# Turning rows into columns on TensorE in the opening of a fused conv and SwiGLU layer

## The chip, the cores and the metric

One NeuronCore of a Trainium2 chip runs the whole kernel as one program. The metric is the device time of one execution in microseconds; the median of the runs is used. The engines named below are TensorE (PE, with its weight loads shown apart as PEld), VectorE (DVE), ScalarE (ACT), GpSimd (POOL) and SyncE (SP), which here only issues DMAs.

## The reference

One layer, in float32, over 2048 tokens of width 1024. `c` is a vector of 1024 that turns into six vectors of shifts, scales and gates.

```python
c_act = silu(c)
sh_m, sc_m, g_m, sh_f, sc_f, g_f = split(c_act @ ada_w + ada_b, 6)
h = rms_norm(x, gain0) * (1 + sc_m) + sh_m          # over the 1024 features of a token
gate_b, gate_c, v = split(h @ w_in, 3)              # 1024 x 3072
h = (gate_b * causal_conv3(gate_c * v)) @ w_out     # 1024 x 1024
x = x + g_m * rms_norm(h, gain1)
h = rms_norm(x, gain2) * (1 + sc_f) + sh_f
g, u = split(h @ w_gate_up, 2)                      # 1024 x 5632
h = (silu(g) * u) @ w_down                          # 2816 x 1024
out = x + g_f * rms_norm(h, gain3)
```

## The kernel before

Features lie on partitions and tokens along the free axis. The 2048 tokens are two units of 1024, and a unit is two halves of 512 tokens (`tok` 0 and 1). Each matrix product is cut into 2 x 2 blocks and done with seven block products P1 to P7 in place of eight (Winograd's form of Strassen). A block product over 512 features is four steps `k` of 128, and a step is three matmuls of 128x512 in the fp32r format: the operands are split into an upper part (`high`, `upper`: a cast on ACT) and a lower part (`low`, `lower`: a subtraction on DVE), and high x high, low x high and high x low are added in PSUM.

The phases follow each other: in0, out0, in1, out1, gu0, down0, gu1, down1. Each phase is a list of slots, a slot being one block product of one group of output features. Work around the slots (loads, sums and splits of weights) is issued by due slots, some slots ahead. All instructions of an engine run in the order in which the program emits them: nothing overtakes on an engine.

The opening, `start()`, is written out by hand, because nothing is on the chip yet. It covers slots 0 to 12 of in0 in pieces and prepares the ones up to 18: P1 of five groups (slots 0 to 4), P2 of five groups (5 to 9), P7 of three (10 to 12); P6 (13 to 15), P5 (16 to 18), P3 and P4 of three groups follow from the general loop. The features of the unit are four tiles of 128 x 4 x 512: `a` and `b` are the lower and upper 512 features of the first token half, `c` and `d` those of the second half. P1 needs `a`, P2 needs `b`, P7 needs `e = a - c`, P6 needs `d - e`, P5 needs `c + d` (in whole fp32 words, without a split).

To make them, `start()` does these steps:

- `load_rows` brings the 512 rows of x of a half; `squares` adds up their squares on ACT; `factor` makes 1/rms of each row (`root`: a power on POOL and three small DVE steps) and puts them on the diagonals of four 128 x 128 blocks (`diagonal`, tile `r0d` or `r1d`); `spread` makes of them, with a product by ones, a tile whose every row holds the factors along the tokens (`rb`).
- `f.load("a")` to `f.load("d")` bring the same rows of x a second time, as columns, from a transposed copy in DRAM (`xt_d`). `mult` multiplies them by `rb` on DVE; `shift` applies scale and shift (`mA`, `mB`) on ACT; `upper` and `lower` split.
- The scales `mA` and shifts `mB` are made in quarters `q` of 256 features. `scales(q, i)` multiplies columns of `ada_w` (128 features on partitions, 1024 inputs along the free axis) by silu(c), spread over the partitions, and adds up along the free axis, in two DVE instructions of 512. `c_half` is that spread c, from two DMAs that read c once for every partition, and `Silu` on ACT. `shifts(q)` does the same sums on TensorE, as a product of one column of silu(c) with 256 features, eight steps; `turned(q)` copies the resulting row to SBUF and turns it into columns with two small transposes. `fold(q)` adds biases and gains.
- `advance("blocks" / "high" / "low" / "sums", i)` takes the loads, casts, subtractions and sums of the weights up to slot i.
- `products(first, ks, ns)` does steps `ks` of slots `first + n`; `follow` takes finished products out of PSUM.

Sixteen tiles of 2 KB a partition hold raw weights, seventeen of 8 KB hold the big operands, and PSUM has eight banks. Nearly every instruction shows line 78 in the profile, since one helper emits them all; rows are told apart by tile names (`in0a` is tile `a`; `ada` columns of ada_w; `ms` the column sums; `pms` the row sums in PSUM; `in0P` either an accumulator or a split weight; `wb` products of ones ahead of the work).

Of the kernel before, what the change touches and what calls it, by code (L numbers as in the profile page):

```python
# [49 lines left out]
def hybrid_conv_layer(  # L50
# [109 lines left out]
    mB = [const.tile([P, KD], F32, name=f"mB{i}") for i in range(2)]  # L160
# [12 lines left out]
    def mods_later(ms, pace):  # L173

        s2 = {(m, h): sb.tile([P, KD], F32, tag="ms", bufs=4, name=f"ms{m}_{h}") for m in ms for h in range(2)}
        for h in range(2):
            half = slice(h * CH, (h + 1) * CH)
            row = raw(f"c{ms[0]}_{h}")
            SP.dma_start(row, c_row[:, half].to_broadcast((P, CH)))
            todo = [(m, n) for m in ms for n in range(KD)]  # L180
            tiles = {}

            def load(i, half=half, todo=todo, tiles=tiles):
                if i < len(todo):
                    m, n = todo[i]
                    tiles[i] = raw(f"ada{m}_{half.start}_{n}")
                    SP.dma_start(tiles[i], ada[m - 1, n][:, half])

            load(0)
            yield pace  # L190
            load(1)
            yield pace
            A.activation(row, row, AF.Silu)
            load(2)
            yield pace
            for i, (m, n) in enumerate(todo):
                load(i + 3)
                t = tiles.pop(i)
                V.tensor_tensor_reduce(t, t, row, 1.0, 0.0, ALU.mult, ALU.add, col(s2[m, h], n))
                yield pace  # L200
# [865 lines left out]
    def start():  # L1066
        ph = phases[0]
        rb, mods, rows, xr = {}, {}, {}, {}
        f = Features(ph, from_xt(0), rb, 0)
        s2 = [sb.tile([P, KD], F32, tag="ms", bufs=4, name=f"ms1_{h}") for h in range(2)]  # L1070
# [9 lines left out]
        def load_scale(q):  # L1080

            t = mods[1, q] = big(f"ada1_{q}")
            for i in range(2):
                SP.dma_start(pair_of(t, i), two(ada[0, 2 * q + i]))
# [7 lines left out]
        sq = {}  # L1092

        def squares(tok, rs):
            if tok not in sq:
                sq[tok] = small(4, f"a{tok}")
            for r in rs:
                t = pair_of(xr[tok][r // 2], r % 2)
                A.activation(t, t, AF.Square, scale=1.0 / 32.0, accum_out=col(sq[tok], r))

        def factor(tok, meanwhile=lambda: None):
# [4 lines left out]
            meanwhile()  # L1106
            return diagonal(at_once(steps), f"r{tok}")

        def shifts(q):
            t = mods[0, q].rearrange("p a b -> p (a b)").rearrange("p (k n) -> p k n", k=KD)  # L1110
            rows[q] = bank(f"pms{q}")
            for k in range(KD):
                PE.matmul(rows[q][0:1, :256], col(cact, k), t[:, k, :], start=k == 0, stop=k == KD - 1)
# [4 lines left out]
        def scales(q, i):  # L1118
            for h in range(2):
                t = mods[1, q][:, 2 * i + h, :]  # L1120
                V.tensor_tensor_reduce(t, t, c_half[h], 1.0, 0.0, ALU.mult, ALU.add, col(s2[h], 2 * q + i))

        def fold(q):
            n = slice(2 * q, 2 * q + 2)
            t = small(2, f"mf{q}")
            V.tensor_tensor(t, s2[0][:, n], s2[1][:, n], ALU.add)
            V.tensor_tensor(t, t, vt[:, VB + KD + n.start : VB + KD + n.stop], ALU.add)
            V.scalar_tensor_tensor(mA[0][:, n], t, 1.0, vt[:, VG + n.start : VG + n.stop], ALU.add, ALU.mult)
            V.tensor_tensor(mB[0][:, n], rows[q][:, :2], vt[:, VB + n.start : VB + n.stop], ALU.add)

        def mult(key, k4):
            t = f.t[key][:, k4, :]
            V.tensor_tensor(t, t, rb[f.place[key][0]], ALU.mult)

        def shift(key, k4):
            t, k = f.t[key][:, k4, :], f.place[key][1] * 4 + k4
            A.activation(t, t, AF.Identity, bias=col(mB[0], k), scale=col(mA[0], k))
# [24 lines left out]
        load_scale(0)  # L1162
        load_shift(0)
        f.load("a")
        advance("blocks", 2)
        load_scale(1)
        load_shift(1)
        advance("blocks", 4)
        f.load("b")
        load_scale(2)  # L1170
        load_shift(2)
        advance("blocks", 7)
        load_shift(3)
        load_rows(1)
        load_scale(3)
        advance("blocks", 9)
        f.load("c")
        advance("blocks", 12)
        f.load("d")
# [12 lines left out]
        for _ in range(6):  # L1192
            PE.matmul(b, one, w, start=True, stop=True)


        squares(0, range(4))
        for h in range(2):
            A.activation(c_half[h], c_half[h], AF.Silu)
        dg = factor(0)
        rb[0] = spread(dg, "r0")  # L1200
        scales(0, 0)
        scales(0, 1)
        shifts(0)
        advance("high", 0)
        for k in range(3):
            mult("a", k)
        turned(0)
        fold(0)
        mult("a", 3)
        advance("low", 0)  # L1210
        for k in range(2):
            shift("a", k)
            upper("A11", k)
            lower("A11", k)
# [3 lines left out]
        scales(1, 0)  # L1218
        scales(1, 1)
        shifts(1)  # L1220
# [3 lines left out]
        turned(1)  # L1224
        fold(1)
        products(4, range(2), range(1))
        split("a", "A11", range(2, 4))
        products(0, range(2, 4))
        for k in range(4):
            mult("b", k)  # L1230
        shifts(2)
        scales(2, 0)
        scales(2, 1)
        products(3, range(2, 4), range(1))
        squares(1, range(2))
        turned(2)
        advance("high", 7)
        products(4, range(2, 4), range(1))
        advance("low", 7)
        squares(1, range(2, 4))  # L1240
        fold(2)
        shifts(3)
        v = small(4, "v1")
        V.tensor_scalar(v, sq[1], EPS, None, ALU.add)
        steps = root(v, "r1")
        next(steps)
        shift("b", 0)
        upper("A12", 0)
        scales(3, 0)
        lower("A12", 0)  # L1250
        shift("b", 1)
        upper("A12", 1)
        scales(3, 1)
        dg = at_once(steps)
        lower("A12", 1)
        turned(3)
        fold(3)
        dg = diagonal(dg, "r1")
        products(5, range(2), range(1))
        rb[1] = spread(dg, "r1")  # L1260
        products(6, range(2), range(1))
        advance("sums", 12)
        shift("b", 2)
        upper("A12", 2)
        mult("c", 0)
        lower("A12", 2)
        mult("c", 1)
        shift("b", 3)
        upper("A12", 3)
        lower("A12", 3)  # L1270
        follow(0, range(3))
        mult("c", 2)
        mult("c", 3)
        products(5, range(2, 4), range(2))
# [5 lines left out]
        products(7, range(4), range(1))  # L1280
        for k in range(4):
            shift("c", k)
# [3 lines left out]
        products(9, range(4), range(1))  # L1286

# [19 lines left out]
        e(3)  # L1307
        advance("low", 12)
        lower("S3", 2)
        lower("S3", 3)  # L1310
        products(10, range(2))
# [4 lines left out]
        for k in range(4):  # L1316
            mult("d", k)
            shift("d", k)
# [149 lines left out]
```

## Time and profile before

| | us |
|---|---|
| median of 3 runs | 1979.15 (1978.1 to 1981.15) |
| the profiled execution | 1980.41 |
| its span on the core | 1978.3 |
| PE busy | 1943.6 (98%) |
| DVE busy | 1465.0 (74%) |
| ACT busy | 869.4 (44%) |

The page splits the span into 40 slices of 49.5 us with one digit for each engine. The opening fills slice 1 and most of slice 2. The windows view gives the same for stretches of one's own choice; the timeline gives every instruction with start, length, and, in brackets, how long its engine had been idle and what ended that.

### The profile page before, as it was taken

The page shows a single profiled execution, that of the slowest core. Times are in us where ns is not written, and L with a number is a line of the kernel's source. Part 1 is how long each engine was busy: PE and PEld are TensorE (multiplying, and loading weights), DVE is VectorE, ACT ScalarE, POOL GpSimd, SP SyncE. Part 2 cuts the span into 40 slices and gives each one's busy share as a digit, 9 for nine tenths or more (in the row PEclk, how much of TensorE's full clock was granted, in tenths as well). Part 3 has the DMA queues.
Part 4 walks back from the last instruction along what each step waited for, and adds up shares of the span by engine and source line. Part 5 has one row for each costly group of instructions (what it writes and reads, how often), then busy time and mean ns, then how long its engine had stood idle before and what let it go on. Part 6 is the DMA issues. An engine that isn't in the chain of part 4 may idle for free.

```text
span 1978.3 us, 24971 instructions
## 1 busy us (share of the span) xinstructions
PE 1943.6 (98%) x8460; PEld 1575.3 (80%) x8460; DVE 1465.0 (74%) x2159; ACT 869.4 (44%) x1428; POOL 344.2 (17%) x224
## 2 busy tenths in 40 slices
PE   7899998999999999999999999999999999999998
PEld 3578886777888888888888888888888888888886
DVE  4898887988999776898776755686776655665466
ACT  4543446544345653443333444463333333344452
POOL 0012201311221211243332320120100100011010
PEclk9999998999999999999999999999999999999999
DMA  9369859859996773777666877577564342386634
GB/s 389 131 226 379 305 172 359 302 201 351 337 317 216 288 261 102 231 246 242 206 223 202 281 285 277 202 261 274 186 197 152 113 154 96 109 310 230 198 138 132
DMA packets 204463, 458.97 MB, mean 232 GB/s; under 512 B 22832, under 2 KB 38320, under 8 KB 197936
## 3 DMA queue, kind: packets, MB, share of 16 engines
q1 hardware_dynamic: 179712, 403.00, 59.3%
q10 hardware_dynamic: 24624, 54.40, 7.2%
q8 instruction: 66, 1.08, 0.2%
q14 instruction: 61, 0.50, 0.1%
HBM read 326.23 MB, written 131.07 MB: 231 GB/s over the span
## 4 chain that ended last, share of the span: by engine, by line
PE 88%; DMA 4%; DVE 4%; issue 2%; ACT 1%; SPq 0%; ACTq 0%; POOL 0%; POOLq 0%; DVEq 0%
PE gu0P L78 21%; PE gu1P L78 21%; PE down0P L78 11%; PE in1P L78 10%; PE in0P L78 10%; PE down1P L78 9%; PE out1P L78 4%; PE out0P L78 1%; DMA ada<-ada_d 1%; DMA in3b<-w_in_d 1%; DMA in0b<-xt_d 0%; DMA ident<-eye_d 0%; DMA in1b<-w_in_d 0%; DVE down1z L78 0%; DMA in2b<-w_in_d 0%
## 5 line engine op out<-in xcount | busy, mean ns | idle before, releaser
L78 DVE TENSOR_TENSOR gu1a<-gu1P,gu1a 128x512 f32<-128x512 f32 x63 | 43.5, 691 | 108.6 <-PE gu1P L78 108.6
L78 DVE TENSOR_TENSOR gu0a<-gu0P,gu0a 128x512 f32<-128x512 f32 x63 | 43.4, 688 | 70.0 <-PE gu0P L78 68.3
L78 POOL TENSOR_TENSOR gu1a<-gu1a 128x512 f32<-128x512 f32 x11 | 19.0, 1728 | 363.5 <-DVE gu1g11s L78 42.5
L78 ACT COPY gu1a<-gu1P 128x512 f32<-128x512 f32 x42 | 24.7, 588 | 98.6 <-PE gu1P L78 87.5
L78 POOL TENSOR_TENSOR nq<-nq,nq 128x512 f32<-128x512 f32 x28 | 42.7, 1525 | 132.8 <-ACT nq L78 128.1
L78 DVE CUSTOM_DVE_ANT_0 ada<-ada,c 128x512 f32<-128x512 f32 x80 | 60.1, 761 | 4.0 <-DMA ada<-ada_d 4.0
L78 ACT COPY gu0a<-gu0P 128x512 f32<-128x512 f32 x42 | 24.5, 587 | 84.6 <-PE gu0P L78 83.5
L78 ACT COPY gu1g<-gu1P 128x512 f32<-128x512 f32 x24 | 14.1, 588 | 92.9 <-PE gu1P L78 92.9
L78 POOL TENSOR_TENSOR down0q<-down0q,down0q 128x512 f32<-128x512 f32 x14 | 23.9, 1704 | 144.1 <-ACT down0q L78 144.0
L78 ACT COPY gu0g<-gu0P 128x512 f32<-128x512 f32 x24 | 14.1, 588 | 77.2 <-PE gu0P L78 77.2
L78 POOL TENSOR_TENSOR gu0a<-gu0a 128x512 f32<-128x512 f32 x11 | 18.3, 1660 | 170.9 <-ACT gu0a L78 50.4
L78 POOL TENSOR_TENSOR down1q<-down1q,down1q 128x512 f32<-128x512 f32 x10 | 16.1, 1610 | 148.7 <-ACT down1q L78 148.6
L78 DVE TENSOR_TENSOR gu1g<-gu1P,gu1g 128x512 f32<-128x512 f32 x24 | 16.6, 691 | 27.5 <-ACT gu1g L78 26.0
L78 DVE TENSOR_TENSOR down2P<-down2P,down2P 128x512 fp32r<-128x512 f32 x14 | 11.9, 853 | 28.6 <-ACT down2P L78 28.6
L78 ACT ACTIVATE gu1a<-gu1a 128x512 f32<-128x512 f32 x42 | 26.6, 633 | 13.4 <-DVE xo L78 6.0
L78 POOL TENSOR_TENSOR out1q<-out1q,out1q 128x512 f32<-128x512 f32 x14 | 22.1, 1579 | 52.3 <-ACT out1q L78 52.3
L78 ACT ACTIVATE gu0a<-gu0a 128x512 f32<-128x512 f32 x42 | 26.6, 632 | 10.4 <-DVE gu0a L78 9.0
L78 POOL TENSOR_TENSOR out0q<-out0q,out0q 128x512 f32<-128x512 f32 x14 | 23.0, 1640 | 46.5 <-ACT out0q L78 46.5
L78 DVE TENSOR_TENSOR xx<-xx,zz 128x512 f32<-128x512 f32 x32 | 29.1, 909 | 1.1
L78 ACT ACTIVATE nq<-xx 128x512 f32<-128x512 f32 x32 | 20.2, 631 | 17.2 <-DVE xx L78 13.9
L78 DVE TENSOR_TENSOR gu0g<-gu0P,gu0g 128x512 f32<-128x512 f32 x24 | 16.5, 689 | 14.4 <-ACT gu0g L78 13.0
L78 ACT ACTIVATE xr<-xr 128x512 f32<-128x512 f32 (+1 forms) x24 | 18.5, 772 | 16.3 <-DMA xr<-x_d 15.3
(3225 smaller groups left out, 6723.5 us busy)
## 6 DMA issues: line engine op xcount, KB each, us to landing
ada<-ada_d SPq DMA_DIRECT2D x64, 256.0 KB, 5.9
act0A<-gu0a SPq DMA_DIRECT2D x33, 256.0 KB, 3.6
act1A<-gu1a SPq DMA_DIRECT2D x33, 256.0 KB, 2.4
ada<-ada_d SPq DMA_DIRECT2D x16, 512.0 KB, 9.4
zz<-z SPq DMA_DIRECT2D x32, 256.0 KB, 5.3
xx<-xt_d SPq DMA_DIRECT2D x32, 256.0 KB, 5.3
x<-xx ACTq DMA_DIRECT2D x32, 256.0 KB, 5.3
down0S<-act0S SPq DMA_DIRECT2D x8, 1024.0 KB, 6.9
```

What stands on the lines that cost most here:

```text
L78: return tc.keep_in_program_order(f(*args, **kwargs))
```

## The change

The opening no longer reads the transposed copy of x, nor c spread from DRAM.

- `turn(key, k)` takes the rows of x as the stationary operand and the diagonal of the factors as the moving one: four products of 128 x 128 x 128 give one step `k` of a feature tile, turned into columns and multiplied by 1/rms, in a PSUM bank. `shift` reads that bank. `mult`, `spread`, `rb` and the loads of `xt_d` in the opening go.
- `spread_c` makes the spread silu(c) with two products by ones.
- `squares` now writes to a tile `junk`, since the rows are needed later; the fourth row tile of a half is squared on DVE (`squares_of_last`).
- The shifts of the first quarter are still done by `shifts(0)` on TensorE, in two parts; those of the other three quarters on DVE with `sums_of(0, n)`, as the scales are with `sums_of(1, n)`. `fold` now goes by single k from k = 2 on. For this `ada_d` holds all six vectors, not five.
- The order of the steps is written anew.

```diff
-    c_half = [tmp(f"c1_{h}")[:, :CH] for h in range(2)]
-    for h in range(2):
-        A.dma_start(c_half[h], c_row[:, h * CH : (h + 1) * CH].to_broadcast((P, CH)))
...
+        def squares_of_last(tok):
+            t, a = pair_of(xr[tok][1], 1), small(2, f"a{tok}h")
+            for h in range(2):
+                V.tensor_tensor_reduce(pair_of(junk, 1)[:, h, :], t[:, h, :], t[:, h, :], 1.0 / 1024.0, 0.0,
+                                       ALU.mult, ALU.add, col(a, h))
+            V.tensor_tensor(col(sq[tok], 3), col(a, 0), col(a, 1), ALU.add)
...
+        def turn(key, *ks):
+            tok, kk = f.place[key]
+            for k in ks:
+                b = turned_x[key, k] = bank(f"x{key}{k}")
+                for r in range(4):
+                    PE.matmul(b[:, r * P : (r + 1) * P], xr[tok][r // 2][:, 2 * (r % 2) + kk, k * P : (k + 1) * P],
+                              dg[tok][:, r * P : (r + 1) * P], start=True, stop=True)
+
+        def spread_c():
+            dg = [diagonal(cact[:, 4 * h : 4 * h + 4], f"c{h}") for h in range(2)]
+            for h in range(2):
+                c_half[h] = tmp(f"c1_{h}")[:, :CH]
+            for h in range(2):
+                b = bank(f"c{h}b")
+                PE.matmul(b, one, dg[h][:, :CH], start=True, stop=True)
+                yield A.copy(c_half[h], b)
...
+        def sums_of(m, n):
             for h in range(2):
+                t = mods[m, n // 2][:, 2 * (n % 2) + h, :]
+                V.tensor_tensor_reduce(t, t, c_half[h], 1.0, 0.0, ALU.mult, ALU.add, col(s2[h], m * KD + n))
+
+        def fold(n0, n1, by_rows=True):
+            g = lambda t: t[:, : 2 * KD].rearrange("p (m n) -> p m n", m=2)[:, int(by_rows) :, n0:n1]
+            V.tensor_tensor(g(mods1), g(s2[0]), g(s2[1]), ALU.add)
+            V.tensor_tensor(g(mods1), g(mods1), g(vt[:, VB : VB + 2 * KD]), ALU.add)
+            V.scalar_tensor_tensor(mA[0][:, n0:n1], mods1[:, KD + n0 : KD + n1], 1.0, vt[:, VG + n0 : VG + n1],
+                                   ALU.add, ALU.mult)
+            if by_rows:
+                V.tensor_tensor(mB[0][:, n0:n1], rows[n0 // 2][:, : n1 - n0], vt[:, VB + n0 : VB + n1], ALU.add)
...
+            A.activation(f.t[key][:, k4, :], turned_x.pop((key, k4)), AF.Identity, bias=col(mB[0], k),
+                         scale=col(mA[0], k))
...
         load_rows(0)
-        load_scale(0)
         load_shift(0)
-        f.load("a")
+        load_columns(1, 0)
         advance("blocks", 2)
...
+        load_columns(1, 3)
+        load_columns(0, 3)
         load_rows(1)
```

The new order of the steps, from the products of ones on (all of it new text; unchanged steps left out after `e`):

```python
        ones(2)
        steps = spread_c()
        squares(0, range(2)); next(steps); squares(0, range(2, 3)); next(steps)
        squares_of_last(0)
        ones(4)
        factor(0)
        shifts(0, range(4)); turn("a", 0); shifts(0, range(4, 8)); turned(0); turn("a", 1, 2)
        sums_of(1, 0); sums_of(1, 1); advance("high", 0); fold(0, 2); advance("low", 0)
        for k in range(2):
            split("a", "A11", (k,)); advance("high", 1 + k); advance("low", 1 + k)
        products(0, range(2)); turn("a", 3)
        advance("high", 4); advance("low", 4)
        products(3, range(2), range(1)); products(4, range(2), range(1))
        for k in range(2, 4):
            sums_of(0, k); sums_of(1, k); fold(k, k + 1, False); split("a", "A11", (k,))
        products(0, range(2, 4)); turn("b", 0, 1)
        sums_of(0, 4); sums_of(1, 4); fold(4, 5, False); shift("b", 0); upper("A12", 0)
        sums_of(0, 5); sums_of(1, 5); lower("A12", 0); fold(5, 6, False); shift("b", 1); upper("A12", 1)
        products(3, range(2, 4), range(1)); advance("high", 7); products(4, range(2, 4), range(1))
        lower("A12", 1); advance("low", 7)
        products(5, range(2), range(1)); turn("b", 2); sums_of(0, 6); sums_of(1, 6)
        products(6, range(2), range(1)); fold(6, 7, False); squares(1, range(2))
        shift("b", 2); upper("A12", 2); sums_of(0, 7); sums_of(1, 7); lower("A12", 2)
        turn("b", 3); fold(7, 8, False); shift("b", 3); upper("A12", 3)
        squares(1, range(2, 3)); lower("A12", 3); squares_of_last(1); factor(1)
        advance("sums", 12)
        products(5, range(2, 4), range(1)); turn("c", 0); shift("c", 0); follow(0, range(3))
        products(6, range(2, 4), range(1)); turn("c", 1); shift("c", 1)
        follow(3, range(2)); advance("high", 9); follow(5, range(1)); advance("low", 8); follow(6, range(1))
        products(7, range(2), range(1)); turn("c", 2, 3); shift("c", 2); shift("c", 3)
        products(7, range(2, 4), range(1)); advance("low", 9)
        products(8, range(4), range(1)); follow(7, range(1)); products(9, range(4), range(1))
        turn("d", 0, 1)
        # e(0) to e(3) as before; then shift("d", 0), shift("d", 1), turn("d", 2, 3),
        # shift("d", 2), shift("d", 3), and on as before without mult("d", k)
```

More of the change, by code (lines that the diff above doesn't have):

```diff
@@ L1217, in start @@
         products(0, range(2))
[L1218 to L1220 removed]
+        turn("a", 3)
         advance("high", 4)
@@ L1241, in start @@
[L1241 to L1258, printed above, removed]
         products(5, range(2), range(1))
-        rb[1] = spread(dg, "r1")
+        turn("b", 2)
@@ L1271, in start @@
+        for _ in factor(1):
+            pass
+        advance("sums", 12)
+        products(5, range(2, 4), range(1))
+        turn("c", 0)
+        shift("c", 0)
         follow(0, range(3))
-        mult("c", 2)
-        mult("c", 3)
-        products(5, range(2, 4), range(2))
+        products(6, range(2, 4), range(1))
+        turn("c", 1)
+        shift("c", 1)
         follow(3, range(2))
```

165 lines of the change are left out of this document (83 added, 82 removed).

## The prediction

> **What bounds the kernel now.** I read the page first (busy shares, then the slices), then the chain of waits, then the windows and the timeline of the first 130 us.
>
> ```profile
> span 1978.3 us, 24971 instructions
> PE 1943.6 (98%) x8460; PEld 1575.3 (80%) x8460; DVE 1465.0 (74%) x2159; ACT 869.4 (44%) x1428; POOL 344.2 (17%) x224
> ...
> PE   7899998999999999999999999999999999999998
> ...
> DVE  4898887988999776898776755686776655665466
> ...
> PEclk9999998999999999999999999999999999999999
> DMA  9369859859996773777666877577564342386634
> ```
>
> TensorE is full except in slices 1, 2 and 7 (and the last): only the opening has idle time to win, and whatever moves the end of the opening moves the end of the run. The windows cut it at three points: 22.33 (the first `mB` written), 55.00 (the diagonal of the second token half written), 92.91 (first product of P5, from which TensorE runs without a gap).
>
> ```profile
> 0.00:22.33 22.33, 13.55 (x32) 4.89 (x32) 7.30 (x30) 8.58 (x15) 1.22 (x5) 0.92 0.93 354
> 22.33:55.00 32.67, 29.27 (x120) 15.90 (x120) 22.11 (x64) 17.38 (x30) 1.38 (x1) 1.00 1.03 417
> 55.00:92.91 37.91, 33.40 (x128) 24.66 (x129) 33.65 (x56) 22.36 (x38) 0.00 (x0) 0.95 0.26 100
> 92.91:130.00 37.09, 36.41 (x139) 25.88 (x138) 35.22 (x50) 18.58 (x27) 1.30 (x1) 1.00 0.43 141
> ```
>
> Columns: PE, PEld, DVE, ACT, POOL busy with instruction counts, clock, DMA share, GB/s. Up to 55 us the DMA engines are full (1.03, 417 GB/s), TensorE has 29.27 of 32.67 and VectorE has a third free; from 55 to 92.91 VectorE is full (33.65 of 37.91); after it TensorE is. So the question is when P5 starts; it was 92.91. I follow the new order up to there.
>
> **Prices.**
>
> ```profile
> 28.19 0.69 DVE L78 CUSTOM_DVE_ANT_0 ada<-ada,c 128x512 f32<-128x512 f32 x1
> 28.80 0.69 DVE L78 CUSTOM_DVE_ANT_0 ada<-ada,c 128x512 f32<-128x512 f32 x1
> 30.62 0.15 DVE L78 TENSOR_TENSOR mf<-ms,ms 128x2 f32<-128x2 f32 x1
> 31.00 0.16 DVE L78 SCALAR_TENSOR_TENSOR mA<-mf,vt 128x2 f32<-128x2 f32 x1
> 39.02 2.49 DVE L78 TENSOR_TENSOR in0b<-in0b,r0r 128x512 f32<-128x512 f32 x4
> 35.34 0.16 DVE L78 TENSOR_TENSOR mB<-pms,vt 128x2 f32<-128x2 f32 x1 [4.18 <-PE pms L78]
> 35.54 0.82 ACT L78 ACTIVATE in0a<-in0a,mB,mA 128x512 f32<-128x512 f32 x1 [1.70 <-DVE mB L78]
> 36.39 0.62 ACT L78 CAST in0A11h<-in0a 128x512 fp32r<-128x512 f32 x1
> 37.04 0.69 DVE L78 TENSOR_TENSOR in0A11l<-in0a,in0A11h 128x512 fp32r<-128x512 f32 x1 [1.53 <-ACT in0A11h L78]
> 29.83 3.62 PE L78 MATMUL pms<-ada,cact 128*1 128x256 f32 x16
> 1960.33 0.95 PE L78 MATMUL lasts<-mean,down1q 128*128 128x1 f32 x8
> 91.55 0.61 PE L78 MATMUL in0P<-in0S2h,in2P 128*128 128x512 f32 x2
> ...
> 92.91 3.59 PE L78 MATMUL in0P<-in0c,in0b 128*128 128x512 f32 x8
> ```
>
> A 128x512 VectorE step follows the last after 0.61 us (28.19 to 28.80), so `sums_of` (two) is 1.22; `fold` without rows 0.55 (30.62 to 31.16); from a fold's end to the start of `lower` 1.54 (35.50 to 37.04: shift, cast, hand-over). One k of a product is three matmuls, 0.68 us. A `turn` of one k is four fp32 products, each two instructions, with 128x128 weights and 128 columns moving. None is in the trace. The bounds: eight loads of 128x128 fp32 weights with one column moving took 0.95 us (`lasts`); fp32 columns stream at 3.59/8 = 0.45 us per 512, so 128 take 0.11, eight 0.9. Hidden loads give 0.95 a turn, loads and streams in a row 1.85. I take 1.0, because in the P7 and P6 products a full 128x128 load fits behind every running matmul:
>
> ```profile
> L78 PEld LDWEIGHTS out0P<-out0S,out1P 128*128 128x128 f32 x16 | 3.0, 188 | 0.6
> ```
>
> 188 ns loads at a matmul every 0.227 us, with no gap. [...]
>
> **Part 1, up to the first mB (was 22.33).**
>
> ```profile
> 2.14 1.01 ACTq L78 DMA_DIRECT2D ident<-eye_d  x1
> 6.06 6.96 PE L78 MATMUL wb<-w,one 128*128 128x512 f32 x12 [6.06 <-DVE w L78]
> 7.93 0.34 PEld L78 LDWEIGHTS wb<-w,one 128*128 128x128 f32 x1 [0.52 <-issue]
> 8.78 0.34 PEld L78 LDWEIGHTS wb<-w,one 128*128 128x128 f32 x1 [0.52 <-issue]
> 11.02 1.06 ACT L78 ACTIVATE xr<-xr 128x1024 f32<-128x1024 f32 x1 [0.70 <-DMA xr<-x_d]
> 12.20 0.17 DVE L78 TENSOR_SCALAR v<-a 128x4 f32<-128x4 f32 x1 [6.19 <-ACT xr L78]
> 12.45 1.02 POOL L78 TENSOR_TENSOR r0p<-v,mhalf 128x4 f32<-128x4 f32 x1 [12.01 <-DVE v L78]
> 14.09 0.88 DVE L78 TENSOR_SCALAR r0d<-ident,r0q 128x128 f32<-128x128 f32 x4
> 16.07 5.26 PE L78 MATMUL pms<-ada,cact 128*1 128x256 f32 x16
> 22.17 0.16 DVE L78 TENSOR_TENSOR mB<-pms,vt 128x2 f32<-128x2 f32 x1 [1.24 <-PE pms L78]
> ```
>
> Removed: the two spread loads of c (512 KB, ACT's queue ahead of `ident`) and 1 MB of xt ahead of the weights: 1.5 MB at 0.42 MB/us is 3.7 us of earlier weights. The last row tile lands about 1.2 us before 11.02. But ACT's new `copy` of the first half of c waits for TensorE: two products of ones at the cold clock (four instructions, their loads 0.85 apart where the end of the 6.96 us runs at 0.43) end at 9.4, the product with c at 10.2, copy 10.8. Behind it on ACT stands the third row's square, done at 12.1. So `v` is at 12.2 as before and the diagonal at 15.05: the earlier rows buy nothing here. VectorE's last-row squares (1.4) lie beside that. TensorE: second half of c to 11.0, four products of ones to 14.5, then warm (3.62 where it took 5.26 cold): half the shifts 1.8, turn a0 1.0, the other half 1.8: 19.1; ACT copy, transposes and mB as before (pms end 21.33 to mB 22.33: 1.0). F, the mB, is at 20.1: **2.2 us earlier**. Bounds: 18.5 if nothing stands in ACT's way, 22 if the shifts run cold. The 512 KB loads not made twice, `load_scale` renamed and `ada[m]` indexed anew cost nothing: same sizes, same queue.
>
> **Part 2, F to the second diagonal (was F + 32.7).** SP's queue holds 4.2 MB less, and the ada columns move up on it, ahead of the weights of P7. At 417 GB/s behind the first 7.9 MB (354 GB/s up to 22.33) the second pair of them has landed at 21, the last at 34, the second rows of x, behind all, at 39; they are needed at 26, 47 and 46. No DMA decides; VectorE, in order, does:
> - `low` 0 to 4, `lower` a0, a1 as before, free at F + 4.6 + 1.2 = 5.85.
> - a2 and a3, each 2.45 (four column sums) + 0.55 + 1.54 waiting + 0.61: 10.3, to 16.15. The wait is new: before, two scales were folded at once; now each k's `lower` stands behind ACT, and the next sums behind it.
> - b0, b1: sums 2.45, fold 0.55, sums 2.45, b0's `lower` (waiting 0.5 for a turn), fold, wait 1.54, `lower`: 25.45. Three `low`: 27.3.
> - b2, b3 likewise: 36.05. Last-row squares 1.4; v, power, root 2.4; diagonal 0.88: F + 40.6.
>
> That is 32 us of work and 8 of waits, against 22.11 busy before: plus six `sums_of` of shift columns (7.3), squares (1.4), folds (1.2), minus five multiplies (2.49 per four). The diagonal comes at 20.1 + 40.6 = 60.7, **5.7 us later**. TensorE loses three sets of shifts (3 x 3.62) and takes five turns (5.0); its 23 us (26 k and the turns) fit in the 40, so it stands idle about 4 us before turn c0, which waits for the diagonal. Queued behind that turn: the second halves of P2, turns c1 to c3, all of P2's last groups; ACT's shift of c0 and the copies behind it wait with it.
>
> **Part 3, to P5 (was 37.9 after the diagonal).** TensorE alone: products 6 (half) to 9, P7, P6 are 38 k at 0.68 = 25.8; eight turns (c, d) 8.0: 33.8. After the idle 4 us it runs slow at first:
>
> ```profile
> 72.94 0.51 PE L78 MATMUL in0P<-in0S3h,in2P 128*128 128x512 f32 x1 [1.80 <-ACT in2P L78]
> ...
> 74.40 1.05 PE L78 MATMUL in0P<-in0S3h,in0P 128*128 128x512 f32 x2
> ```
>
> After 1.8 us of waiting two matmuls took 1.05 instead of 0.61, for some 4 us; that is 2 us lost: 35.8. [...] VectorE, rid of eight multiplies and of its waits, ends S2's last `lower` at F + 68.5 and c + d with its sums (6.6) at 75.2, before P5. P5 starts at 60.7 + 35.8 = 96.5 against 92.91: **+3.6 us**, the sum of -2.2, +7.9 and -2.1. Behind P5 TensorE is the bound as before (36.41 of 37.09), so the end moves by the same.
>
> The profiled execution took 1980.41 (span 1978.3), 1.3 above the median 1979.15; on the median +3.6 gives 1982.7. Something like 0.2% (4 us) is what a measurement of this kernel can tell from no change.
>
> **Rivals.**
> - *Weight loads not hidden* (a turn 1.85): turn a0 before mB +0.85, eight turns behind the diagonal +6.8, the others in TensorE's slack. 1982.7 + 7.6 = 1990. For it: no row shows full loads with short streams; against: the 188 ns loads hidden above.
> - *Faster: loads were the bound.* If the DMA's 1.03 up to 55 us held VectorE back, and the ada loads' early landing lets column sums fill the waits ahead of `lower`, the 8 us of waits in part 2 go: the diagonal at 52.7, TensorE waits less and stays warm. P5 at 52.7 + 33.8 = 86.5, 6 us before, 1973. It decides once the diagonal is ahead of 55. Against it: the order on VectorE is fixed, and `lower` stands ahead of the next sums.
> - *Slow clock more often.* TensorE also waits about 2.2 us before a3 and 1.8 before b3; if each costs 2 us on the path, 1986.
> - *Hidden on both sides:* F at 18.5 and no cold stretch: 1982.7 - 1.6 - 2 = 1979, inside the forecast's range.
>
> **How the numbers follow.** The forecast with its own range (1979 to 1986) has 0.5, of which 0.36 lies within 0.2% and 0.14 above; loads not hidden 0.2, slow clock 0.14, both slower; the faster rival 0.16. So faster 0.16, same 0.36, slower 0.48; the forecast stands just inside the same band. The range runs from 1974, near the faster rival, to 1990.
>
> **What would show it.** Right: the eight instructions of a turn take about 1.0 us; first mB near 20; the second diagonal near 60 with TensorE idle before turn c0 on DVE r1d; DMA share falling from 1.0 by 45 us; P5's first product near 96. Wrong: turns of 1.8; the diagonal ahead of 56; P5 ahead of 91; or a change behind P5, where I expect none.

## The result and the profile after

The change made the kernel slower by 0.63%: median 1990.39 us (1988.81 to 1993.96, four runs) against 1978.87 for the kernel before in the same session, ratio 1.0063, 95% interval 1.0051 to 1.0074. The profiled execution took 1991.1, its span 1988.9, which is 10.6 above the span before.

The page of the kernel after, its busy shares and slices:

```profile
span 1988.9 us, 25149 instructions
PE 1946.7 (98%) x8534; PEld 1587.0 (80%) x8534; DVE 1467.1 (74%) x2191; ACT 864.3 (43%) x1419; POOL 345.6 (17%) x224
...
PE   7799998999999999999999999999999999999998
...
DVE  6698778978999876798776755687776665565466
...
PEclk9899999999999999999999999999999999999999
DMA  9149859869996783687566777668564242386544
```

TensorE has a 7 in slice 2 where it had an 8, and slice 2 is now the one with the lower clock. VectorE went from 4 and 8 to 6 and 6 in the first two slices. The DMA share of slice 2 fell from 3 to 1, so fewer bytes move, as meant. TensorE's busy time rose by 3.1 in all; the other 7.5 us of the span are idle time.

The windows, cut at the same three events as before (first `mB` written, turn c0, which waits for the second diagonal, first product of P5), with the same columns:

```profile
21.03:61.19 40.16, 28.80 (x135) 21.27 (x133) 30.18 (x93) 17.96 (x29) 1.01 (x1) 0.93 0.69 266
61.19:104.24 43.05, 38.42 (x178) 31.36 (x179) 29.71 (x49) 19.36 (x33) 0.00 (x0) 0.91 0.15 56
104.24:141.33 37.09, 36.41 (x139) 25.89 (x138) 34.79 (x51) 19.29 (x27) 1.46 (x1) 1.00 0.45 147
```

The first stretch took 21.03 instead of 22.33 (1.3 won), the second 40.16 instead of 32.67 (7.5 lost), the third 43.05 instead of 37.91 (5.1 lost): P5 starts 11.3 later. The last row is what it was before, so nothing more is lost behind P5. Neither new stretch is full on any engine: in the second TensorE works 28.80 and VectorE 30.18 of 40.16, in the third 38.42 and 29.71 of 43.05. In the second stretch the loss is waiting: TensorE stands idle for 11.36 us of it where it stood idle for 3.40. In the third it stands idle for 4.63, hardly more than the 4.51 before; what grew there is its busy time, by 5.0, with the eight turns of `c` and `d` in it and a lower granted clock (0.91 instead of 0.95).

What VectorE waited for between 21 and 61.2 in the kernel after (in total, times, longest):

```profile
DVE in0A11l L78 <- ACT in0A11h L78: 4.5, 4, 1.6
DVE in0A12l L78 <- ACT in0A12h L78: 3.6, 3, 1.6
DVE mods L78 <- PE pms L78: 2.4, 1, 2.4
DVE r1t L78 <- POOL r1p L78: 1.1, 1, 1.1
```

The first two are the hand-overs to ACT and back in front of each `lower`, 8.1 us. The third ends with the first `mB` and belongs to the first stretch.

TensorE's timeline from the second diagonal on (start, length, and in brackets the idle time before and what ended it); the turns and the first products of P7 and P6:

```profile
61.19 2.05 PE L78 MATMUL xc<-r1d,xr 128*128 128x128 f32 x8 [3.25 <-issue]
...
70.17 1.16 PE L78 MATMUL xc<-r1d,xr 128*128 128x128 f32 x8 [1.27 <-ACT in0c L78]
...
78.01 2.84 PE L78 MATMUL xd<-r1d,xr 128*128 128x128 f32 x24
...
82.52 1.16 PE L78 MATMUL xd<-r1d,xr 128*128 128x128 f32 x8 [1.67 <-ACT in0d L78]
83.44 0.70 PE L78 MATMUL in0P<-in0S3h,in0P 128*128 128x512 f32 x2
...
91.80 0.73 PE L78 MATMUL in0P<-in0S2h,in0P 128*128 128x512 f32 x2
...
94.33 0.50 PE L78 MATMUL in0P<-in0S2l,in0P 128*128 128x512 f32 x1 [0.84 <-DVE in0S2l L78]
...
96.14 0.73 PE L78 MATMUL in0P<-in0S2l,in0P 128*128 128x512 f32 x1 [0.85 <-DVE in0S2l L78]
96.67 1.06 PE L78 MATMUL in0P<-in0S2h,in0P 128*128 128x512 f32 x2
...
104.24 3.59 PE L78 MATMUL in0P<-in0c,in0b 128*128 128x512 f32 x8
```

Four things are to be seen. Turn c0 comes after 3.25 idle and takes 2.05, at a granted clock of 0.50 (from 59 to 65.5). Three turns in a row are 24 instructions in 2.84, 0.95 a turn. Turns c3 and d3 wait 1.27 and 1.67 for ACT, not for data: ACT's shift reads the PSUM bank of an earlier turn, and there is no other bank. And P6, which should be as long as P7 (83.44 to 91.80, 8.36), takes 12.44, with two waits for the lower part of S2.

The other side of that last wait, on ACT and VectorE of the kernel after:

```profile
87.21 0.62 ACT L78 CAST in0P<-in0b 128x512 fp32r<-128x512 f32 x1 [2.71 <-DMA kin3P<-in3P]
88.91 0.62 ACT L78 CAST in1P<-in1b 128x512 fp32r<-128x512 f32 x1 [1.07 <-DMA kin4P<-in4P]
90.61 0.62 ACT L78 CAST in2P<-in2b 128x512 fp32r<-128x512 f32 x1 [1.08 <-PE in0P L78]
91.13 1.14 ACT L78 CAST in0S2h<-in0a 128x512 fp32r<-128x512 f32 x2
...
91.78 0.69 DVE L78 TENSOR_TENSOR in0S2l<-in0a,in0S2h 128x512 fp32r<-128x512 f32 x1 [3.22 <-ACT in0S2h L78]
```

Three casts of P6's weights stand on ACT ahead of the casts of S2: VectorE had written the data of the first two of S2's by 86.21 (84.92 and 1.29), and ACT began them at 91.13. The first two wait for stores of weights (`kin3P`, `kin4P`) that leave the buffers they write to, the third for TensorE to be done with a P7 weight buffer. (ACT issues these stores itself, the last of them from 85.48 to 87.11, and an issue does not count as busy; so the first of the two waits can as well be the issuing.) VectorE stands 3.22 behind them, and TensorE then waits for VectorE.

### The profile page after: what moved, and what is told of

It reads as the page before. It is cut to its first block, busy times and chain, and to the rows that moved or that the text cites. A ratio compares the mean times of both kernels' runs of the same rounds, so it can differ in the third digit from the quotient of the medians.

```text
span 1988.9 us, 25149 instructions
## 1 busy us (share of the span) xinstructions
PE 1946.7 (98%) x8534; PEld 1587.0 (80%) x8534; DVE 1467.1 (74%) x2191; ACT 864.3 (43%) x1419; POOL 345.6 (17%) x224
## 4 chain that ended last, share of the span: by engine, by line
PE 86%; DVE 7%; issue 3%; DMA 3%; ACT 2%; POOL 0%; POOLq 0%; ACTq 0%; DVEq 0%; SPq 0%
PE gu0P L78 21%; PE gu1P L78 21%; PE in0P L78 11%; PE down0P L78 11%; PE in1P L78 9%; PE down1P L78 9%; PE out1P L78 3%; DVE ada L78 1%; DMA ada<-ada_d 1%; DVE in1y L78 0%; DVE in1c L78 0%; PE wb L78 0%; DMA out0S<-y0S 0%; DMA xr<-x_d 0%; DVE down1z L78 0%
## 5 line engine op out<-in xcount | busy, mean ns | idle before, releaser
L78 DVE CUSTOM_DVE_ANT_0 ada<-ada,c 128x512 f32<-128x512 f32 x92 | 67.6, 752 | 3.7 <-DMA ada<-ada_d 3.7
L78 DVE TENSOR_TENSOR down10P<-down10P,down10P 128x384 fp32r<-128x384 f32 x14 | 7.8, 556 | 21.1 <-ACT down10P L78 21.1
```

What stands on the lines that cost most here:

```text
L78: return tc.keep_in_program_order(f(*args, **kwargs))
```

## The experiments

My theory after the result: the time is lost to the order in which engines take their work, and not to the work. VectorE waits ahead of `lower`, and behind the diagonal TensorE waits for PSUM banks and for casts queued on ACT. The rivals: sums of the shifts on VectorE are simply too much for it; the turns themselves cost the time; or the saved loads matter, one way or the other. Ratios are to the kernel before, with 95% intervals. Times of a place in the trace come from one execution each. The times of one kernel spread by 1.2 to 5 us, so differences of 1 us are read from the place and not from the medians.

**Shifts back on TensorE, turns kept.**

```diff
-        load_columns(0, q)             # q = 1 to 3
+        load_shift(q)
-            sums_of(0, k); sums_of(1, k); fold(k, k + 1, False); split("a", "A11", (k,))
+        shifts(1); sums_of(1, 2); sums_of(1, 3); turned(1); fold(2, 4); split("a", "A11", range(2, 4))
```

and likewise for the other quarters (shown without the steps that stand between).

> The changed kernel with the shifts of the last three quarters back on TensorE (rows of products with c, as in the kernel before) and folds by pairs; x is still turned by TensorE. Theory 1 (up to turn c0 VectorE's order decides): VectorE loses 7.3 us of sums and two of the waits behind a fold (3 us), so the second diagonal comes 7 to 10 us before 61.2, and P5 5 to 8 us before 104.2, although TensorE gets 3 x 3.62 us more; time 1983 to 1986. Theory 2 (TensorE's own new work, the turns, is what costs): 10.9 us more on TensorE make it slower still, 1994 to 2001. Theory 3 (it is the loads, or the loss lies behind P5): within 2 us of the changed kernel.

Measured: 1996.75, ratio 1.0095 (1.008 to 1.011). By theory 1 it was expected to be faster; it is slower still, at a time that theory 2 gave. The windows from 20 to 61 of this kernel and of the kernel after:

```profile
20.00:61.00 41.00, 38.64 (x190) 24.82 (x190) 21.01 (x57) 19.61 (x34) 0.00 (x0) 1.00 0.70 271
```

```profile
20.00:61.00 41.00, 29.37 (x137) 21.77 (x136) 30.15 (x93) 18.84 (x31) 1.01 (x1) 0.93 0.70 270
```

With the turns on it, TensorE has no room for the shifts' row sums (38.64 of 41 busy), and VectorE waits for them instead: its waits for `pms` grow from 2.4 to 10.9. So beside the turns, moving the shifts to VectorE is a gain of 6.4 us, and that the sums are too much work for VectorE falls. For the kernel after, where TensorE works 29.37 of the same 41 us, this run does not tell theory 1 from theory 2; the next one does.

**The waits filled.** The next column sums are put between the cast and `lower`:

```diff
-            sums_of(0, k); sums_of(1, k)
+            if k == 2: sums_of(0, k); sums_of(1, k)
             fold(k, k + 1, False)
-            split("a", "A11", (k,))
+            shift("a", k); upper("A11", k)
+            sums_of(0, k + 1); sums_of(1, k + 1)
+            lower("A11", k)
...
+        sums_of(0, 6); sums_of(1, 6)
         lower("A12", 1)
...
-        lower("A12", 3)
         squares_of_last(1)
+        lower("A12", 3)
```

> The changed kernel with the same work, but the column sums of the next k (and the squares of the last row tile) stand ahead of lower on VectorE, so that four waits of 1.54 us (a2, a3, b1, b3) are filled. Theory 1: the second diagonal comes 4 to 6 us earlier (55 to 57), TensorE's wait before turn c0 shrinks, P5 4 to 6 us earlier, 1984 to 1986.5. Theory 2 (the turns cost it) and theory 3 (loads, or behind P5): no change, 1990 within 2 us.

Measured: 1984.57, ratio 1.0041 (1.0026 to 1.0055), 5.8 below the kernel after. VectorE's waits in this kernel up to 56, and TensorE at the diagonal:

```profile
DVE in0A11l L78 <- ACT in0A11h L78: 1.4, 2, 0.9
DVE in0A12l L78 <- ACT in0A12h L78: 1.4, 1, 1.4
```

```profile
55.38 2.04 PE L78 MATMUL xc<-r1d,xr 128*128 128x128 f32 x8 [2.07 <-issue]
```

The hand-overs fall from 8.1 to 2.8 and turn c0 comes 5.8 earlier, at 55.38: the waits were most of the second stretch's loss of 7.5, and theory 2, by which nothing would change here, falls. P5 starts at 96.13, 8.1 earlier; most of what comes on top of the 5.8 is the clock: P6 took 10.82 in this execution instead of 12.44, with no pair in it above 0.73.

**P6's third cast behind S2's, in the kernel after and in the kernel before.** The same edit in both:

```diff
-        advance("high", 15)
+        advance("high", 14)
         for k in range(4):
             ...
-            if k: advance("low", 12 + k); lower("S2", k - 1)
+            if k: (advance("low", 12 + k) if k < 3 else None); lower("S2", k - 1)
         lower("S2", 3)
+        advance("low", 15)
```

> The changed kernel with one cast moved: the upper part of P6's third weight, which waits for a weight buffer that P7 holds, goes behind the casts of S2 on ACT instead of ahead of them. Theory 4 (the 12.4 us that P6 takes for 8.2 us of matmuls come from that cast: S2's casts and VectorE's lower stand behind it): P6 runs in 8.2 to 9 us and P5 starts 3.5 to 4.2 us earlier; 1986 to 1987. Rival (VectorE's own work of about 8 us for S2 sets it): under 1 us.

> The same move in the kernel before, where P6 took 10.8 us (82.1 to 92.9). Theory 4: P6 in 8.2 to 9 us, P5 2 to 2.6 us earlier, 1976.3 to 1977. So the stall is common to both kernels and not of the change's making. Rival: no change, 1979 within 1 us.

Measured in the kernel after: 1987.22, ratio 1.0047 (1.0032 to 1.0062), 3.2 less than without the edit. P6 there takes 8.62 instead of 12.44. In the kernel before: 1977.34 (1976.3 to 1977 was expected), ratio 0.9994 (0.9985 to 1.0003), which is not told from no change. Its P6 takes 9.08 where it took 10.83. First products of P6 and P5, in the one and in the other:

```profile
90.58 0.62 PE L78 MATMUL in0P<-in0S2h,in0P 128*128 128x512 f32 x2
```

```profile
80.94 0.62 PE L78 MATMUL in0P<-in0S2h,in0P 128*128 128x512 f32 x2
...
90.02 3.59 PE L78 MATMUL in0P<-in0c,in0b 128*128 128x512 f32 x8
```

(P5 of the first starts at 99.20.) So most of this stall was in the kernel before as well; the change did not make it. What the kernel after has more, 1.6 (12.44 against 10.83), lies in the slow clock at 96.14 (granted 0.56 from 96 to 98 and 0.59 from 98 to 100, where the kernel before has 1.00 in the whole of P6). The two waits of 0.84 and 0.85 ahead of it are also in the kernel with the loads made again (below), at 92.85 and 94.66, with no slow stretch behind them, and 10.81 for the whole of P6. So it is not shown that these 1.6 belong to the change.

**Banks freed earlier.** ACT's casts of weights go behind the shifts that read the banks, and shifts d0 and d1 go ahead of `e(2)`:

```diff
-        advance("high", 9)
         follow(5, range(1))
-        advance("low", 8)
         follow(6, range(1)); products(7, range(2), range(1))
-        turn("c", 2, 3); shift("c", 2); shift("c", 3)
+        turn("c", 2); shift("c", 2); turn("c", 3); shift("c", 3); advance("high", 9); advance("low", 8)
...
+        shift("d", 0); shift("d", 1)
         e(2); advance("high", 12); e(3)
-        shift("d", 0); shift("d", 1)
```

> The changed kernel with two hand-overs of PSUM banks made earlier: shift c2 ahead of turn c3 and of two weight casts on ACT, and shifts d0 and d1 ahead of the casts of e(2) and e(3). Theory 5 (turns c3 and d3 waited 1.3 and 1.7 us because five banks stay with the groups and a turn must wait until ACT has emptied an earlier turn's bank): both waits go, P7 starts 2 to 3 us earlier after turn c0 (22.3 us between them before), P5 too; 1987.4 to 1988.5. Rival (ACT or VectorE is late there anyway, another wait takes their place): under 1 us.

Measured: 1988.39, ratio 1.0051 (1.0036 to 1.0066). The median is 2.0 lower, not told from the kernel after by itself. In the trace both bank waits are gone and four turns run as one block (`xd` 32 instructions in 3.73); turn c0 is at 61.18 as in the kernel after, and P7 begins at 80.73 instead of 83.44:

```profile
80.73 0.71 PE L78 MATMUL in0P<-in0S3h,in0P 128*128 128x512 f32 x2
```

**TensorE kept busy ahead of turn c0.**

```diff
+        for _ in range(3):
+            PE.matmul(bank("ww"), one, w)     # results not used
         turn("c", 0)
```

> The changed kernel with three products by ones (2.6 us, results unused) ahead of turn c0, where TensorE waits 3.2 us for the second diagonal. Theory 6 (the idle time drops the clock, and turn c0 and the six matmuls behind it lose 2.2 us by it): turn c0 takes 1.0 instead of 2.05 us, P7 and P5 come 2 to 2.3 us earlier, 1988.2. Rival (VectorE or the banks set the pace behind the diagonal): under 1 us although the clock stays up.

```profile
57.66 2.73 PE L78 MATMUL ww<-w,one 128*128 128x512 f32 x6
61.07 1.13 PE L78 MATMUL xc<-r1d,xr 128*128 128x128 f32 x8 [0.67 <-PE ww L78]
```

Measured: 1989.09, ratio 1.0055 (1.004 to 1.007). Turn c0 takes 1.13 instead of 2.05, and P7 starts 20.23 behind it instead of 22.25: the cold clock cost the 2 us that were forecast. The median shows 1.3 of it, within its uncertainty.

**The loads made again.** The opening loads of `xt_d` go back to their old places, 4 MB to a DRAM tile that nothing reads:

```diff
         load_shift(0)
+        SP.dma_start(scratch("xa"), xt_d[...])    # and three more, at the places of f.load
```

> The changed kernel with the four 1 MB loads of the transposed x issued again at their old places in SP's queue, into a scratch area that nobody reads. Theory 7 (the 4.2 MB that the change saves buy nothing, since no wait of the changed opening ends with a load): 1990 to 1991.5, P5 at most 1.5 us later, and that through the first weights, which the load of a delays. Rival (the saved loads are worth what part 1 gained or more): 3 to 6 us slower.

Measured: 1990.40, ratio 1.0061 (1.0044 to 1.0078): the same as without them. From 21 to 61 us the DMA share is 0.93 where the kernel after has 0.69, and yet turn c0 is no later (60.10). What the change took off the queue bought no time, and for the changed kernel the rival that the loads were the bound falls.

**The weights' stores issued ahead of shift d0.**

```diff
         e(3)
+        passed(10)
         shift("d", 0)
...
         products(10, range(2, 4))
-        passed(10)
```

> The changed kernel with ACT's four stores of kept weights issued ahead of the shifts of d, as they stood in the kernel before, not behind them. The casts of P6's first two weights waited 2.7 and 1.1 us for those stores. Theory 4 (the third cast, which waits for P7, decides): the two waits go but P6 starts and runs as it did; under 0.7 us. Rival (the stores hold up P6): P6 in under 10 us instead of 12.4, 2 to 3 us faster.

Measured: 1991.89, ratio 1.0067 (1.0052 to 1.0082): no gain. ACT's waits for the stores are gone and P6 takes 8.16, but ACT's issues now stand ahead of the shifts, so turn d3 waits longer for its bank, and P7 starts later and, with pairs of 1.06 behind that wait, takes 9.87:

```profile
84.65 1.16 PE L78 MATMUL xd<-r1d,xr 128*128 128x128 f32 x8 [3.75 <-ACT in0d L78]
85.57 0.70 PE L78 MATMUL in0P<-in0S3h,in0P 128*128 128x512 f32 x2
...
95.44 0.61 PE L78 MATMUL in0P<-in0S2h,in0P 128*128 128x512 f32 x2
```

Both expectations missed a part: P6 ran as the rival said and not as theory 4 did, and the time did not fall. The stall only moved: with the issues ahead of the shifts on ACT's queue, turn d3 waited 3.75 for its bank where it had waited 1.67.

**The squares ahead of the spread of c.**

```diff
         ones(2)
+        squares(0, range(3))
         steps = spread_c()
-        squares(0, range(2)); next(steps); squares(0, range(2, 3)); next(steps)
+        next(steps); next(steps)
         squares_of_last(0)
-        ones(4)
+        ones(1)
```

> The changed kernel with the third square of the first half ahead of the copies of the spread c on ACT, and one product of ones behind it instead of four. Theory 8 (in part 1 the new copies on ACT, which wait for TensorE, hold up the square and so the first diagonal): the first diagonal 1.5 to 2 us earlier (14.6 before), the first mB at 18.5 to 20 instead of 21.0, all behind it as much earlier; 1988.5 to 1989.5. Rival (TensorE's cold clock or the load of ada0 sets mB): mB not earlier than 20.5.

```profile
16.93 0.16 DVE L78 TENSOR_TENSOR mods<-pms,vt 128x2 f32<-128x2 f32 x1 [1.09 <-PE pms L78]
```

Measured: 1988.98, ratio 1.0059 (1.0043 to 1.0074). The first diagonal is begun at 11.94 instead of 14.59, and the first `mB` comes 4 us earlier than in the kernel after (17.09, ahead of the 18.5 to 20 expected), turn c0 also (57.22). But the edit does two things, and the 4 us are not the price of the square alone: it also leaves out three products of ones ahead of the shifts. The last products of ones in the kernel after, then in this one:

```profile
11.71 3.60 PE L78 MATMUL wb<-w,one 128*128 128x512 f32 x8
```

```profile
10.35 1.02 PE L78 MATMUL wb<-w,one 128*128 128x512 f32 x2
```

In the kernel after TensorE works without a gap up to the end of the shifts, and turn a0 starts at 17.05, 1.6 behind the diagonal: there its own row of work sets `mB` and not the square. Of the 4 us, 2.6 are the products of ones, 0.9 the two products that spread c (2.63 there, from 9.08 to 11.71, and 1.72 here, from 8.63 to 10.35; that this is the clock is an estimate from these times alone), and 0.5 an earlier start. Without the square moved, though, turn a0 would have to wait for the diagonal at 15.47, so the edit needs both its parts; what each is worth by itself was not run.

In the profiled execution P5 comes 4.8 earlier (99.41) and the span is 3.5 shorter, but this is the fastest of four (1987.94 to 1991.38); the median falls by only 1.4, and why the others gain less stays open.

**All of it.** The filled waits, the casts, the banks and two warming products together; then the same with the squares first; then a third order with the second rows' squares and factor right behind P2's first steps, so that the diagonal comes as early as it can. The first two put diffs shown above together (with two warming products, not three); of the third, the core of what is new:

```diff
+        squares(1, range(3))
         products(5, range(2), range(1)); turn("b", 2)
-        products(6, range(2), range(1))
+        squares_of_last(1); half = factor(1); next(half)
...
-        products(5, range(2, 4), range(1)); turn("c", 0); shift("c", 0); follow(0, range(3))
-        products(6, range(2, 4), range(1)); turn("c", 1); shift("c", 1)
+        turn("c", 0); shift("c", 0); products(5, range(2, 3), range(1))
+        turn("c", 1); shift("c", 1); products(5, range(3, 4), range(1)); products(6, range(4), range(1))
```

> The waits on VectorE filled, P6's third cast behind S2's, the two bank hand-overs earlier, and two products by ones ahead of turn c0, together. If the terms found one by one are the whole of part 2 and 3 and add up (5.8 + 3.2 + 2.0 + 1.3): 1978, the time of the kernel before. If they overlap (each shortens a wait that another one hides): 1981 to 1984.

> The same with the third square first as well: 1 to 2 us less than with the four edits alone, if theory 8 holds; then 1976 to 1977, under both kernels. Otherwise as those.

> Waits filled, P6's cast moved, d's shifts early and the third square first, and the second half's squares and diagonal now right behind the first steps of P2, so that the turns of c run in the time in which TensorE waits for VectorE. If, as theory 1 says, VectorE's order decides up to turn c0 and TensorE has idle time there: no wait of over 2 us ahead of turn c0, P5 at 86 to 90 (92.9 in the kernel before), 1972 to 1976. If TensorE's work is the bound: as the version with all four edits.

| | median | ratio | turn c0 | P5 |
|---|---|---|---|---|
| before | 1978.35 | | (second diagonal 55.00) | 92.91 |
| all | 1977.21 | 0.9994 (0.9986 to 1.0003) | 54.72 | 89.68 |
| all, squares first | 1976.64 | 0.9991 (0.9983 to 1.0000) | 53.27 | 88.26 |
| early diagonal | 1978.06 | 1.0002 (0.9993 to 1.0010) | 49.48 | 90.17 |

The separate terms add up: 13.2 us come back with the first, 13.7 with the second. So with the turns and all the sums still in it, another order of the steps and two warming products take the loss away. The second is the best version and is below the kernel before by 0.09%, at the edge of what can be told; against the kernel before with P6's cast moved as well (1977.34) it is not shown to be faster.

The third missed 1972 to 1976: the diagonal is 4 us earlier, yet P7 is not (72.83 against 70.90). From turn c0 to P7 TensorE is busy for 21.91 of 23.35 us, where with the squares first it was 17.40 of 17.63: more of P2 is left behind the earlier turn (119 instructions instead of 106), and with no warming products the clock fell behind the wait of 1.99 ahead of it (0.93 instead of 1.00 in this stretch). There TensorE's work is the bound, the other case of the expectation.

Nor does an earlier P5 come through in full: with the squares first P5 starts 4.65 before that of the kernel before, and the span is 3.2 shorter. The windows from 200 to 300, this kernel and the kernel before:

```profile
200.00:300.00 100.00, 98.10 (x430) 80.24 (x428) 75.65 (x138) 41.81 (x88) 13.45 (x9) 1.00 0.69 233
```

```profile
200.00:300.00 100.00, 100.00 (x441) 82.42 (x440) 81.24 (x144) 44.33 (x93) 14.00 (x10) 1.00 0.71 237
```

TensorE is busy for 1.9 us less there, where before it was full; only 0.8 of it is a wait on record, for VectorE. But from P5 to the end the fifteen traces of this case take between 1884.1 and 1887.2, the kernel before 1885.4 and this one 1886.8, with no order in it by when P5 starts. So 1.4 us more behind P5 is no more than these traces differ by anyhow.

**The sums alone, on the kernel before.** No turns; the shifts of three quarters on VectorE:

```diff
-        shifts(q); turned(q)              # q = 1 to 3
+        shift_sums(q)                     # four sums of 512 columns each, on VectorE
```

> The kernel before with the other half of the change alone: x still loaded twice and multiplied on VectorE, but the shifts of the last three quarters summed on VectorE and not on TensorE. If the sums on VectorE are what costs: VectorE gets 7.3 us more and the time goes up by 4 to 7 us, 1982 to 1985. If the turns on TensorE are what costs, and the sums on VectorE only make room for them: TensorE loses 10.9 us, VectorE had ten us of waits for mB in which the sums fit, the second diagonal stays at 52 to 57 and the time within 3 us of 1978.3.

Measured: 1980.25, ratio 1.0007 (0.9998 to 1.0016). The window 21 to 55:

```profile
21.00:55.00 34.00, 21.69 (x68) 13.67 (x69) 30.48 (x93) 16.18 (x27) 1.38 (x1) 0.79 1.03 417
```

VectorE works 30.48 in 34, about as much as it does in 40.16 of the kernel after, and the time hardly moves: where its order leaves no waits it has the room. So the four corners are: neither part, 0; sums alone, +1.3 (not told from nothing); turns alone, +18.4; both, +11.5. (Turns alone is the run with the shifts back on TensorE; the rest of the change, such as c spread by TensorE, is in it too.) The turns bring the loss, by the order that was written around them, and the sums take part of it back.

## Why the prediction was wrong

The forecast was 1982.7, slower by 3.6; measured is +11.5 (1990.39). The direction was right, the size not, and the step that failed is part 3: the 33.8 us of TensorE "alone", which put the waits from the second diagonal to P5 at nothing.

**Part 1, first `mB` at 20.1; measured 21.03.** Two prices were too low. The product that spreads c at the cold clock was put at 0.8 (9.4 to 10.2); it took 1.91 (and 1.02 in the run with the squares first):

```profile
9.08 1.91 PE L78 MATMUL c0b<-c0d,one 128*128 128x512 f32 x2
...
11.03 0.58 ACT L78 COPY c<-c0b 128x512 f32<-128x512 f32 x1 [3.79 <-PE c0b L78]
11.51 1.06 ACT L78 ACTIVATE junk<-xr 128x1024 f32<-128x1024 f32 x1
```

With that the four products of ones began at 11.71 instead of 11.0; and the shifts with turn a0 between them took 4.8 (15.23 to 20.03) instead of 4.6. ACT's queue was read rightly: the third square stands behind the copy and sets the diagonal, written at 15.47 (forecast 15.05). As in the forecast's own sum, it is TensorE's row of work that ends in `mB`.

**Part 2, F + 40.6; measured F + 40.16.** Right to half a us, and in its mechanism: VectorE's order decides, TensorE stands idle before turn c0 (about 4 forecast, 3.25 measured), and no DMA decides. The filled waits showed it. The total is closer than its parts: 32 us of work and 8 of waits were forecast, and VectorE worked 30.18 and stood idle 9.98. The work does not follow from its own list either: 22.11 with what is added and taken off there is 28.9.

**Part 3, "TensorE alone: [...] 33.8", with 2 for the cold clock; measured 43.05 against 35.8.** The cold clock was right (P7 started 2.0 sooner behind turn c0 with the warming products). The rest was priced as a queue of TensorE work that waits for nobody. The forecast had read VectorE as full in this stretch of the kernel before, at 33.65 of 37.91; among the 4.3 us that it stood idle there is its wait for ACT's cast of S2, which P6 then pays for (1.22, shown below).

- Two bank waits, 1.27 + 1.67 = 2.9. The forecast did not count PSUM banks: five accumulators stay live from P1 through P6, and three of eight banks are left for the accumulators of P2 and all turns.
- P6 at 8.2 instead of 12.44, 4.3. VectorE was said to end S2's last `lower` at F + 68.5, which is 88.6; it ended at 96.7. The forecast charged VectorE's own work and left out the ACT queue between: stores, three weight casts, then S2's casts. The trace before held the warning, for its P6 lasted 10.83 (82.08 to 92.91), with the same two waits in it (below), and the forecast priced P6 by matmul count. So 2.6 of the 4.3 are a stall that the change inherited. About 1.6 is the clock, which fell there in this execution and in that of the shifts back on TensorE (12.43), but not with the filled waits, the banks, the warming products, the loads made again and the squares first (10.81 to 10.86).

P6 in the kernel before, on VectorE and TensorE:

```profile
82.06 0.69 DVE L78 TENSOR_TENSOR in0S2l<-in0a,in0S2h 128x512 fp32r<-128x512 f32 x1 [1.22 <-ACT in0S2h L78]
...
82.08 0.73 PE L78 MATMUL in0P<-in0S2h,in0P 128*128 128x512 f32 x2
...
84.61 0.50 PE L78 MATMUL in0P<-in0S2l,in0P 128*128 128x512 f32 x1 [0.84 <-DVE in0S2l L78]
...
86.42 0.50 PE L78 MATMUL in0P<-in0S2l,in0P 128*128 128x512 f32 x1 [0.85 <-DVE in0S2l L78]
```

Up to P5 the errors are 0.9 in part 1, -0.4 in part 2 and 7.2 in part 3, 7.7 in all; P5 was forecast at 96.5 and came at 104.24.

**Behind P5** the forecast of no change holds: 11.3 at P5, 10.6 in the span.

**The rivals.** "Weight loads not hidden" gave 1990, the number measured, by a mechanism that is not there: three turns in a row take 0.95 each, the value of the lower bound (24 instructions with full 128-row weights in 2.84 us, 0.118 each). "Loads were the bound" fell with the loads made again. "Slow clock more often" came true in two places. One is the first that it named: behind a wait of 2.59 at 36.77 a pair took 1.05 (granted clock 0.55 from 38 to 40), but TensorE had idle time there, and VectorE, which sets the pace in that stretch, waited no more than 0.44 for b0 behind it. The other, at 96.14, is a place where the forecast did not look.

## What to carry to other kernels

When work is moved to an engine that has room, write down each queue that the new order passes and each buffer or bank that it needs, with who frees it: here VectorE had the room, and what cost time was hand-overs with nothing behind them (turn c0 5.8 earlier without them), three free PSUM banks (P7 2.7 earlier), casts ahead of casts on ACT (P6 8.62 instead of 12.44), and the slow clock behind the waits (2.0 at turn c0). Price a stage by its length in the profile before and not by its instruction count; where the two differ (P6: 10.83 against 8.2) there is already a wait in it that the change will inherit or enlarge. A load taken off a queue bought nothing here (1990.39 without the loads and 1990.40 with them), where from the first `mB` on no wait of VectorE or TensorE ended with a load; look for that wait first.

## What the runs showed of the hardware

- A product of 128x128x128 in fp32 is two instructions of 0.118 us when it follows others of its kind, with a full weight load beside each (24 instructions in 2.84 us, their 24 loads in 2.87 us of the same stretch); a single turn stands at 1.05 to 1.16 where the granted clock is 1.00.
- Behind waits of 2.07 and 3.25 us turn c0 took 2.04 and 2.05, against 1.13 after dummy products; in the kernel after the granted clock was 0.50 from 59 to 65.5 us. Behind a wait of 2.67 us in the run with the squares first (33.32) the pairs took 0.62 to 0.74, as at full clock. Behind two waits of 0.84 and 0.85 us the clock fell in the kernel after (pair 1.06 at 96.67, granted 0.53 from 96.14 to 98) and stayed up in the kernel before with the same waits (pair 0.63 at 86.75, granted 1.00). How long a wait has to be for it, the runs do not show.
